# Low parts, half-length convolution filters and per-token roots in a split-float32 hybrid layer

## The chip, the cores and the metric

The kernel runs on one core of a Trainium2 chip. The metric is device time in microseconds (us) of one execution. TensorE (PE in the profile) multiplies matrices into PSUM, which has eight banks of 128 x 512 float32 here. VectorE (DVE), ScalarE (ACT) and GpSimd (POOL) work element by element. SyncE (SP) issues most DMAs; GpSimd issues those that add while they copy. Each engine takes its instructions strictly in the order in which they were written.

## The reference

One layer over x, 1024 tokens x 1024 channels, all float32:

```python
u = x @ w_in + b_in                      # q k v z_att glu_a glu_b z_conv g_att g_conv
att = stick_breaking_attention(q, k, v)  # 8 heads of 64, strictly causal
att_branch = (att * silu(z_att)) @ w_att_proj
c = causal_depthwise_conv(glu_a * sigmoid(glu_b), conv_w) + conv_b   # 31 taps, 512 channels
c = silu(layer_norm(c, conv_ln_g, conv_ln_b))
conv_branch = (c * silu(z_conv)) @ w_conv_proj + b_conv_proj
y = (sigmoid(g_att) * att_branch + sigmoid(g_conv) * conv_branch) @ w_out
return layer_norm(2 ** 0.25 * x + y, ln_g, ln_b)
```

`att_branch`, `conv_branch` and both gates have 1024 channels, everything else in the branches has 512.

## The kernel before

Channels lie on partitions and tokens along the free axis (tiles of 128 x 1024, "blk"; half tiles of 128 x 512, "hf"). A float32 product is made of three faster ones: each operand is split into a rounded high part (`wh`, `xh`) and the rest, the low part (`wl`, `xl`), and `mm3` (lines 190 to 193) issues high x high, high x low, low x high for each 128-channel slice. A weight piece is 128 x 512; `feed` keeps at most `N_SPL` = 5 split pieces at once, so a piece can be split at most four pieces before its use. ScalarE makes `wh` (line 216). The low part is made in one of three ways: VectorE or GpSimd subtracts, or ScalarE writes minus `wh` (line 222) and GpSimd issues a DMA that adds the weight from memory (line 223).

The order of work: the values of the attention (pieces 0 to 7), then attention units on TensorE with the input projection's remaining pieces (8 to 53, "dense work") laid between them, then `p12` pieces (36 to 39, 42, 43 and 54 to 67). The two gates and z_conv, 20 column blocks of w_in, go in ten pairs; each pair is a seven-product scheme. Two products use plain weights (`p12`), the other five (`P5 P6 P7 P4 P3`, pieces 68 to 117, results in `sps`) use sums and differences that `make_s` forms on VectorE: S1, then S2 from S1, then S4 from S2, all in the same half tile `s`, and S3; A22 is plain. `split_operand` (line 899 issues the DMA) splits them; `DMA_LOW` names those whose low part is made by the adding DMA. Each of `pair_out`'s sums is a VectorE addition that reads PSUM and frees a bank. Then follow the attention's projection (pieces 118 to 125, operands `ach`, `acl`), the convolution's (126 to 133, operands `cch`, `ccl`) and the output projection.

In the dense work VectorE also does the depthwise convolution: `conv_block` has one 128 x 1024 instruction per tap (line 387, 31 for each of four channel blocks). When all blocks are done `conv_norm` sums over channels on TensorE (lines 601, 602, `mps` and `vps`, each source split into two parts first), and takes the reciprocal root of the variance as 128 x 1024, the same on every partition. `ev_qk` evacuates q and k of a head in two halves of 64 partitions each.

What sets the order is a planner: `Timeline` holds a price per engine and instruction; `tl.run` writes each instruction of VectorE, ScalarE and GpSimd into its queue when the planner's clock says that the engine is free, by rank (convolution taps have rank 9, last). The order is fixed when the program is built; on the chip only semaphores act.

Of the kernel before, what the change touches and what calls it, by code (L numbers as in the profile page):

```python
# [9 lines left out]
F32 = mybir.dt.float32  # L10
# [4 lines left out]
P = 128  # L15
# [3 lines left out]
H = 8  # L19
# [22 lines left out]
DMA_LOW = ("A22", "S3", "S4")  # L42

A_LOW, C_LOW, O_LOW = "V", "G", "V"

# [10 lines left out]
GUARD = 150  # L56

# [100 lines left out]
def layer_kernel(ctx: ExitStack, tc, xT, x, wv, wd, wa, wc, wo, vec, bv, lng, lnb, cst, out):  # L158
# [30 lines left out]

    def mm3(ps, wh, wl, mh, ml, first, last):  # L190
# [7 lines left out]
    epsc = const.tile([P, 1], F32, name="epsc")  # L198
    ones = const.tile([P, P], F32, name="ones")
# [86 lines left out]
    def run_dense():  # L286
        for n_item, (first_piece, npc, mov, evac, may, nhf) in enumerate(items):
            dstat["item"] = n_item
            nk = 4 * npc
            if mov is None:  # L290
# [4 lines left out]
                for k in range(nk):  # L295
                    if k % 4 == 0:
                        while live["ps"] >= 8:
                            tl.skip()
                        ps = bank("dps")
                    pi = first_piece + k // 4  # L300
                    need(pi)
                    wh, wl = parts[pi]
                    kk = slice((k % 4) * P, (k % 4 + 1) * P)
                    mm3(ps, wh[:, kk], wl[:, kk], xh[k][:, 0:HALF], xl[k][:, 0:HALF], k % 4 == 0, k % 4 == 3)
                    tl.t += 3 * pe_ns(HALF)
                    if k % 4 == 3:
                        parts.pop(pi)
                        stat["free"] += 1
                        feed()
                        evac(ps, None if k == 3 else ps)  # L310
                    yield
            for half in range(2 if mov is not None else 0):
# [6 lines left out]
                for k in range(nk):  # L319
                    pi = first_piece + k // 4  # L320
                    need(pi)
                    wh, wl = parts[pi]
                    kk = slice((k % 4) * P, (k % 4 + 1) * P)
                    mh, ml = mov(k)
                    mm3(ps, wh[:, kk], wl[:, kk], mh[:, cols], ml[:, cols], k == 0, k == nk - 1)
                    tl.t += 3 * pe_ns(HALF)
                    if half == 1 and k % 4 == 3:
# [3 lines left out]
                    if k == nk - 1:  # L331
# [57 lines left out]
    def ev_qk(h):  # L389
        def f(half, cols, ps):  # L390
            if half == 0:
                qhh[h], qll[h], ks[h] = (blk(f"{n}{h}", F32R) for n in ("qhh", "qll", "ks"))
                qk_left[h] = [6, 2, 0.0]
            else:
                qk_left[h][1] = 2
            lo, up = slice(0, DH), slice(DH, P)
            a, b, c = qhh[h], qll[h], ks[h]
            left = qk_left[h]
            mine = [2]

            def fin(e):
                left[0] -= 1
                left[2] = max(left[2], e)
                if left[0] == 0:
                    qk_ready[h] = left[2]

            def read(e):
                mine[0] -= 1
                if mine[0] == 0:
                    drop("ps")  # L410

            def dup():
                fin((yield act(2, a[up, cols], f32(a[lo, cols]))))

            def q():
                e = yield act(0, a[lo, cols], ps[lo], AF.Identity, bias=vcol(h, lo))
                tl.spawn(dup(), e)
                e = yield vstt(0, b[lo, cols], ps[lo], vcol(h, lo), f32(a[lo, cols]), ALU.add, ALU.subtract)
                read(e)
                fin((yield act(2, b[up, cols], f32(b[lo, cols]))))  # L420

            def k():
                yield act(0, c[up, cols], ps[up], AF.Identity, bias=vcol(h, up))
# [933 lines left out]
```

## Time and profile before

| | |
|---|---|
| median of 3 runs | 794.17 us (790.4 to 795.58) |
| profiled execution | 791.7 us, span 789.8 us |
| PE busy | 749.3 us (95%) |
| DVE busy | 659.5 us (83%) |
| ACT busy | 398.4 us (50%) |
| POOL busy | 107.5 us (14%) |
| DMA moved | 109.55 MB |

A matmul's busy time contains its way through the array, so matmuls overlap and a busy share of 95% hides idle time; the spacing of their starts tells more. On DVE and ACT, too, an instruction's recorded time reaches into the next one's. The span has five stages: values (0 to 60 us), attention with dense work (60 to 340), the rest of the dense work (340 to 400), `p12` and the pairs (400 to 620, where the attention's projection begins near 601), the projections and the output (620 to the end).

### The profile page before, as it was taken

How to read it: one execution, taken by the hardware profiler on the slowest of the kernel's cores; microseconds unless marked ns; L12 is line 12 of the kernel's file. 1: busy time of each engine (PE TensorE's matmuls, PEld its weight loads, DVE VectorE, ACT ScalarE, POOL GpSimd, SP SyncE). 2: the span in 40 equal slices, each digit the busy share in tenths (PEclk: the TensorE clock that was granted, in tenths of full speed). 3: DMA queues.
4: the chain of work that ended last, by engine and by line, in shares of the span. 5: the costliest groups of instructions: out<-in, count | busy, mean ns of one | idle time of the engine just before them, and what ended most of it. 6: DMA issues, size and time to landing. Idle time of an engine off the chain costs nothing.

```text
span 789.8 us, 10242 instructions
## 1 busy us (share of the span) xinstructions
PE 749.3 (95%) x3606; PEld 624.0 (79%) x3606; DVE 659.5 (83%) x877; ACT 398.4 (50%) x747; POOL 107.5 (14%) x176
## 2 busy tenths in 40 slices
PE   9999999999999999999998989888977999999995
PEld 7887888888878888888876777667765888888885
DVE  7456989999999999979999998989899858920885
ACT  2159865975587898725525353346655334300100
POOL 3212001110110111011212111111110022100000
PEclk9999999999999999999999999999999999999998
DMA  7535125222432334396769767767667777140052
GB/s 245 159 67 117 33 40 107 54 55 54 109 78 50 85 79 114 70 298 186 199 148 247 187 170 175 201 179 193 158 155 258 263 245 260 68 173 0 1 187 80
DMA packets 49730, 109.55 MB, mean 139 GB/s; under 512 B 5520, under 2 KB 6416, under 8 KB 49680
## 3 DMA queue, kind: packets, MB, share of 16 engines
q1 hardware_dynamic: 36864, 85.77, 32.0%
q0 software_dynamic: 12672, 23.07, 18.1%
q8 instruction: 28, 0.46, 0.2%
q14 instruction: 22, 0.18, 0.1%
q10 hardware_dynamic: 144, 0.07, 0.0%
HBM read 84.24 MB, written 19.40 MB: 131 GB/s over the span
## 4 chain that ended last, share of the span: by engine, by line
PE 62%; issue 13%; DVE 13%; DMA 5%; ACT 4%; POOL 2%; SPq 0%; POOLq 0%; DVEq 0%; ACTq 0%
PE dps L192 10%; PE dps L191 10%; PE dps L193 10%; PE vps L1116 6%; PE yps L192 4%; PE yps L193 4%; PE yps L191 4%; DVE cacc L387 4%; PE pvps L754 4%; PE tps L731 3%; DMA wl<-s 3%; PE sps L193 2%; PE sps L191 2%; PE sps L192 2%; DVE f L713 2%
## 5 line engine op out<-in xcount | busy, mean ns | idle before, releaser
L193 PE MATMUL dps<-xh,wl 128*128 128x512 f32 x400 | 156.9, 392 | 5.0 <-DMA wl<-wd 5.0
L191 PE MATMUL dps<-xh,wh 128*128 128x512 f32 x400 | 157.8, 395 | 0.0
L192 PE MATMUL dps<-xl,wh 128*128 128x512 f32 x400 | 156.6, 392 | 0.0
L387 DVE SCALAR_TENSOR_TENSOR cacc<-cin,vecs,cacc 128x1023 f32<-128x1023 f32 (+24 forms) x120 | 148.1, 1270 | 0.7
L223 POOL DMA_DIRECT2D wl<-wd x58 | 50.4, 869 | 318.4 <-ACT wl L222 254.1
L193 PEld LDWEIGHTS dps<-xh,wl 128*128 128x128 f32 x400 | 75.4, 189 | 22.1 <-DMA wl<-wd 5.9
L713 DVE TENSOR_TENSOR_SCAN f<-f,eyez 128x896 f32<-128x896 f32 (+3 forms) x64 | 84.5, 1344 | 3.4 <-ACT f L381 3.4
L192 PEld LDWEIGHTS dps<-xl,wh 128*128 128x128 f32 x400 | 75.6, 189 | 14.0
L191 PEld LDWEIGHTS dps<-xh,wh 128*128 128x128 f32 x400 | 75.5, 189 | 13.8
L216 ACT ACTIVATE wh<-wr 128x512 fp32r<-128x512 f32 x84 | 53.2, 633 | 63.4 <-DMA wr<-wv 25.1
L192 PE MATMUL yps<-wol,mh 128*128 128x512 f32 (+1 forms) x136 | 51.2, 377 | 0.0
L193 PE MATMUL yps<-woh,ml 128*128 128x512 f32 (+1 forms) x136 | 51.2, 376 | 0.0
L191 PE MATMUL yps<-woh,mh 128*128 128x512 f32 (+1 forms) x136 | 51.2, 376 | 0.0
L381 ACT ACTIVATE wth<-tps 128x384 fp32r<-128x384 f32 (+1 forms) x80 | 41.4, 563 | 17.1 <-PE tps L731 15.6
L384 DVE TENSOR_TENSOR wtl<-tps,wth 128x384 fp32r<-128x384 f32 (+1 forms) x80 | 47.1, 627 | 2.9 <-ACT wth L381 2.5
L381 ACT ACTIVATE f<-zps 128x384 f32<-128x384 f32 (+2 forms) x96 | 45.0, 515 | 4.9 <-PE zps L699 4.4
L384 DVE TENSOR_TENSOR b<-b,f 128x895 f32<-128x895 f32 (+3 forms) x64 | 46.7, 747 | 0.3
L387 DVE SCALAR_TENSOR_TENSOR xrow<-xrow,yps 128x512 f32<-128x512 f32 (+1 forms) x17 | 10.7, 655 | 43.0 <-PE yps L193 42.7
L381 ACT ACTIVATE b<-zps 128x383 f32<-128x383 f32 (+2 forms) x96 | 46.0, 529 | 0.3
L220 POOL TENSOR_TENSOR wl<-wr,wh 128x512 fp32r<-128x512 f32 x18 | 25.8, 1434 | 106.0 <-ACT wh L216 101.1
L754 PE MATMUL pvps<-wth,v 128*128 128x256 f32 (+1 forms) x160 | 40.0, 279 | 0.0
L754 PE MATMUL pvps<-wtl,v 128*128 128x256 f32 (+1 forms) x160 | 39.8, 286 | 0.2 <-DVE wtl L384 0.2
(173 smaller groups left out, 1658.3 us busy)
## 6 DMA issues: line engine op xcount, KB each, us to landing
wl<-wd POOLq DMA_DIRECT2D x68, 256.0 KB, 4.8
wr<-wd SPq DMA_DIRECT2D x60, 256.0 KB, 3.1
rc<-wd SPq DMA_DIRECT2D x20, 512.0 KB, 7.2
c<-c SPq DMA_DIRECT2D x30, 256.0 KB, 2.8
ga<-c SPq DMA_DIRECT2D x8, 512.0 KB, 5.5
wor<-wo SPq DMA_DIRECT2D x16, 256.0 KB, 4.5
gc<-c SPq DMA_DIRECT2D x8, 512.0 KB, 5.6
xrow<-x SPq DMA_DIRECT2D x8, 512.0 KB, 6.5
```

The lines of the kernel that those rows point to most:

```text
L191: nc.tensor.matmul(ps, wh, mh, start=first, stop=False)
L192: nc.tensor.matmul(ps, wh, ml, start=False, stop=False)
L193: nc.tensor.matmul(ps, wl, mh, start=False, stop=last)
L216: yield "A", 1, HALF, lambda: nc.scalar.activation(wh, r, AF.Copy)
L220: e = yield "G", 0, HALF, lambda: nc.gpsimd.tensor_tensor(wl, r, f32(wh), op=ALU.subtract)
L223: e = yield "G", 0, 0, lambda: nc.gpsimd.dma_start(wl, src, accum_op=ALU.add), {"extra": 430}
L381: return "A", u, n, (lambda: nc.scalar.activation(out, in_, func, **kw)), (BIAS if "bias" in kw else {})
L384: return "V", u, n, lambda: nc.vector.tensor_tensor(out, a, b, op=op)
L387: return "V", u, n, (lambda: nc.vector.scalar_tensor_tensor(out, a, s, b, op0, op1)), (PTR if ptr else {})
L713: yield ("V", 2, n, lambda: nc.vector.tensor_tensor_scan(f[:, 0:n][:, ::-1], f[:, 0:n][:, ::-1], eyez[:, S - n:S][:, ::-1], 0.0, op0=ALU.mult,
L754: nc.tensor.matmul(u.ps[:, 0:n], st, wt[:, jj * 256:jj * 256 + n], start=(i == m and jj == 0 and wt is wh), stop=(i == 0 and jj == 1 and w ...
L1116: nc.tensor.matmul(vps[tb], a[k][:, tt], b, start=k == 0 and j == 0, stop=k == NK - 1 and j == 2)
```

## The change

Eight edits are made together. `DMA_LOW` becomes empty and VectorE makes the low parts of all pair operands; the same holds for the last 14 plain pieces before the pairs (54 to 67, `N_TURN`). `mm_piece` takes the place of `mm3` in the projections: per piece first the eight products with `wh`, then the four with `wl`. `ev_qk` makes one high and one low part for q and k together on 128 partitions, then four copies of 64 partitions. The convolution runs on even and odd tokens: three half-length filters (even tokens with 16 even taps, odd tokens with 15 odd taps, their sum with the 16 sums of neighbouring taps, which are made once in `hs_`), from which the two output halves are combined; `cin` and `cacc` hold the even tokens in the first half. The norm's channel sums use unsplit float32 matmuls; the variance is summed per token (8 matmuls of one column), the root is taken on 128 x 8, and 8 diagonal tiles and two matmuls spread it over the partitions again (`rps`). `LAG` shifts these sums by 8 us on the planner's clock. Two GLU items move ahead of `p12` item 2, and the last two pairs are interleaved.

```diff
-DMA_LOW = ("A22", "S3", "S4")
+DMA_LOW = ()
+N_TURN, T_LOW = 14, "V"
+LAG = 8000
...
+    def mm_piece(ps, wh, wl, movs, first, last):
+        ks = [slice(k * P, (k + 1) * P) for k in range(4)]
+        for kk, (mh, ml) in zip(ks, movs):
+            nc.tensor.matmul(ps, wh[:, kk], mh, start=first and kk is ks[0], stop=False)
+            nc.tensor.matmul(ps, wh[:, kk], ml, start=False, stop=False)
+            tl.t += 2 * pe_ns(HALF)
+            yield
+        for kk, (mh, ml) in zip(ks, movs):
+            nc.tensor.matmul(ps, wl[:, kk], mh, start=False, stop=last and kk is ks[3])
...
         j = i - (len(pieces) - 2 * NK)
+        if 0 < items[n_pairs[0]][0] - len(pair_order) - i <= N_TURN:
+            return T_LOW
...
-            def q():
-                e = yield act(0, a[lo, cols], ps[lo], AF.Identity, bias=vcol(h, lo))
-                tl.spawn(dup(), e)
-                e = yield vstt(0, b[lo, cols], ps[lo], vcol(h, lo), f32(a[lo, cols]), ALU.add, ALU.subtract)
...
-            def k():
-                yield act(0, c[up, cols], ps[up], AF.Identity, bias=vcol(h, up))
-                e = yield vstt(0, c[lo, cols], ps[up], vcol(h, up), f32(c[up, cols]), ALU.add, ALU.subtract)
...
+            def g():
+                yield act(0, a[:, cols], ps, AF.Identity, bias=vcol(h))
+                yield vstt(0, b[:, cols], ps, vcol(h), f32(a[:, cols]), ALU.add, ALU.subtract)
+                drop("ps")
+                yield [act(2, c[up, cols], f32(a[up, cols])), act(2, c[lo, cols], f32(b[up, cols]))]
+                e = yield [act(2, a[up, cols], f32(a[lo, cols])), act(2, b[up, cols], f32(b[lo, cols]))]
...
-        yield "V", 9, S, lambda: nc.vector.tensor_scalar(a, c, w(0), vcol(CONVB + i), op0=ALU.mult,
-                                                         op1=ALU.add), {"per": 0.521}
-        for sh in range(1, TAPS):
-            yield vstt(9, a[:, sh:], c[:, :S - sh], w(sh), a[:, sh:], ALU.mult, ALU.add, S - sh, ptr=False)
...
+        def run(x, taps, y, prep=None):
+            if prep is not None:
+                yield prep
+            for m, h in enumerate(taps):
+                if m == 0:
+                    yield "V", 9, HALF, lambda: nc.vector.tensor_scalar(y, x, h, None, op0=ALU.mult), {"per": 0.521}
+                else:
+                    yield vstt(9, y[:, m:], x[:, :HALF - m], h, y[:, m:], ALU.mult, ALU.add, HALF - m, ptr=False)
...
+        def last():
+            yield vtt(9, b[:, ev], b[:, ev], a[:, ev], ALU.subtract)
+            yield vtt(9, a[:, 1:HALF], a[:, 1:HALF], a[:, HALF:S - 1], ALU.add, HALF)
+            yield vtt(9, a[:, od], b[:, ev], a[:, od], ALU.subtract)
+            yield "V", 9, S, lambda: nc.vector.tensor_scalar(a, a, vcol(CONVB + i), None, op0=ALU.add), {"per": 0.521}
...
+        tl.spawn(run(c[:, ev], [w(2 * m) for m in range(n)], a[:, ev]), tl.now)
+        tl.spawn(run(c[:, od], [w(2 * m + 1) for m in range(n - 1)], a[:, od]), tl.now)
+        tl.spawn(run(b[:, od], [hsum[:, m:m + 1] for m in range(n)], b[:, ev],
+                     vtt(9, b[:, od], c[:, ev], c[:, od], ALU.add)), tl.now)
...
-                nc.tensor.matmul(ps, ones_r, h[:, c], start=True, stop=False)
-                nc.tensor.matmul(ps, ones_r, l[:, c], start=False, stop=True)
+                nc.tensor.matmul(ps, ones, src[:, c], start=True, stop=True)
...
+                nc.tensor.matmul(ps[:, b:b + 1], q[:, b * P:(b + 1) * P], ones[:, 0:1], start=b == 0, stop=b == NT - 1)
...
-        yield "V", 1, S, lambda: nc.vector.reciprocal(r, sd), {"per": 6.2}
+        yield "V", 1, NT, lambda: nc.vector.reciprocal(r, sd), {"per": 6.2}
...
+        yield [("V", 1, P, (lambda b=b: nc.vector.tensor_scalar(dg[:, b * P:(b + 1) * P], ident, r[:, b:b + 1], None,
+                                                               op0=ALU.mult)), {"per": 0.521}) for b in range(NT)]
+        yield lambda: got.extend(total(dg, "rps"))
...
-    pair_order = [(q, n) for n in range(len(pairs)) for q in ("P5", "P6", "P7", "P4", "P3")]
+    n2 = len(pairs) - 2
+    pair_order = [(q, n) for n in range(n2) for q in ("P5", "P6", "P7", "P4", "P3")] + \
+        [(q, n) for qs in (("P5", "P6"), ("P7", "P4", "P3")) for n in (n2, n2 + 1) for q in qs]
...
-    p12_item(2)
-    att_done = lambda: flags["att"]
-    glu_item(2, lambda: heads_z_done(H - 1))
+    att_done = lambda: flags["att"]
+    z_done = lambda: heads_z_done(H - 1)
+    glu_item(2, z_done)
+    glu_item(3, z_done)
+    p12_item(2)
     zatt_item(3)
-    glu_item(3, att_done)
...
+        taps = vecs[:, w0:w0 + TAPS][:, ::-1]
+        nc.vector.tensor_tensor(hsum[:, 0:TAPS // 2], taps[:, 0:TAPS - 1:2], taps[:, 1:TAPS:2], op=ALU.add)
+        nc.vector.tensor_copy(hsum[:, TAPS // 2:], taps[:, TAPS - 1:TAPS])
```

How instructions move is shown at three places. First TensorE at piece 72, the first `P3` (operand S4; `xh`, `xl` are the split input). Before:

```order
L191 MATMUL sps_4630<-xh4_289,wh72_4529 128x512
L192 MATMUL sps_4630<-xl4_290,wh72_4529 128x512
L193 MATMUL sps_4630<-xh4_289,wl72_4530 128x512
L191 MATMUL sps_4630<-xh5_319,wh72_4529 128x512
L192 MATMUL sps_4630<-xl5_320,wh72_4529 128x512
L193 MATMUL sps_4630<-xh5_319,wl72_4530 128x512
```

and now:

```order
L199 MATMUL sps_4709<-xl6_363,wh72_4609 128x512
L198 MATMUL sps_4709<-xh7_392,wh72_4609 128x512
L199 MATMUL sps_4709<-xl7_393,wh72_4609 128x512
L203 MATMUL sps_4709<-xh4_290,wl72_4610 128x512
L203 MATMUL sps_4709<-xh5_320,wl72_4610 128x512
L203 MATMUL sps_4709<-xh6_362,wl72_4610 128x512
```

`wl72` was read by the third matmul of the piece and is read by the ninth now.

Second, GpSimd's queue at the turn from the dense work to the pairs. Before, it issues an adding DMA for each plain piece and for three of five pair operands:

```order
L223 DMA wl65_4352<-wd 128x512
L223 DMA wl66_4377<-wd 128x512
L223 DMA wl67_4404<-wd 128x512
L899 DMA wl70_4478<-rc25_3726 128x512
L899 DMA wl71_4503<-wd 128x512
L899 DMA wl72_4530<-s0_3729 128x512
L899 DMA wl75_4603<-rc27_4014 128x512
```

and now:

```order
L242 DMA wl51_3991<-wd 128x512
L242 DMA wl52_4017<-wd 128x512
L242 DMA wl53_4087<-wd 128x512
L239 TENSOR_TENSOR wl126_6071<-wr126_6006,wh126_6070 128x512
L239 TENSOR_TENSOR wl127_6124<-wr127_6075,wh127_6123 128x512
L239 TENSOR_TENSOR wl128_6169<-wr128_6096,wh128_6168 128x512
```

From piece 54 to piece 125 GpSimd has no low part to make; its queue has 121 rows where it had 165.

Third, VectorE at the first pair (`s0` holds S1, S2, S4 in turn; `rc24`, `rc25` are the pair's raw weights; `cacc`, `cs` are convolution sums). Before:

```order
L384 TENSOR_TENSOR wl69_4454<-s0_3729,wh69_4453 128x512
L387 SCALAR_TENSOR_TENSOR cacc3_4219<-cin3_4129,vecs_75,cacc3_4219 128x1014
L384 TENSOR_TENSOR c11_8_4486<-dps_4457,p1_8_4461 128x512
L384 TENSOR_TENSOR s0_3729<-rc24_3725,s0_3729 128x512
L387 SCALAR_TENSOR_TENSOR cacc2_3930<-cin2_3857,vecs_75,cacc2_3930 128x1004
```

and now:

```order
L396 TENSOR_TENSOR wl69_4535<-s0_3770,wh69_4534 128x512
L399 SCALAR_TENSOR_TENSOR cs3_4410<-cs3_4410,hs__77 128x508
L396 TENSOR_TENSOR s0_3770<-rc24_3766,s0_3770 128x512
L396 TENSOR_TENSOR c11_8_4566<-dps_4537,p1_8_4540 128x512
L396 TENSOR_TENSOR wl70_4560<-rc25_3767,wh70_4559 128x512
L399 SCALAR_TENSOR_TENSOR cacc3_4409<-cin3_4068,vecs_75,cacc3_4409 128x506
L399 SCALAR_TENSOR_TENSOR c11_8_4566<-c11_8_4566,vecs_75,zg200_4573 128x512
L399 SCALAR_TENSOR_TENSOR cacc3_4409<-cin3_4068,vecs_75,cacc3_4409 128x506
L396 TENSOR_TENSOR wl71_4583<-rc25_3767,wh71_4582 128x512
```

The low parts 70, 71 (and 72) are new in the queue; the taps are half as long, and the convolution's block 3, the only one still open, stands at about the sixth tap of each filter, where before blocks 2 and 3 stood at taps 20 and 10 of 30.

## Rows read from the trace of the kernel before

**Rows 1.** Busy time by window: step, then PE, PEld, DVE, ACT, POOL busy (instructions), granted clock, DMA share, GB/s.

```profile
60.00:340.00 280.00, 277.27 (x1551) 239.96 (x1550) 266.58 (x332) 215.93 (x451) 34.07 (x100) 1.00 0.35 78
340.00:400.00 60.00, 60.00 (x267) 49.67 (x266) 52.33 (x59) 25.49 (x40) 10.41 (x12) 1.00 0.80 224
400.00:620.00 220.00, 192.35 (x809) 152.26 (x808) 198.07 (x245) 105.99 (x170) 33.08 (x38) 0.98 0.72 194
620.00:780.00 160.00, 160.00 (x726) 133.26 (x725) 101.74 (x176) 31.22 (x55) 12.36 (x8) 1.00 0.39 137
440.00:520.00 80.00, 72.17 (x309) 56.86 (x308) 69.76 (x90) 31.34 (x55) 13.00 (x15) 1.00 0.70 181
```

**Rows 2.** Waits of TensorE: who waited for what, us in total, times, the longest.

```profile
PE sps L193 <- DMA wl<-s: 12.3, 8, 4.6
PE dps L193 <- DMA wl<-wd: 5.0, 2, 3.9
PE dps L192 <- DVE acl L384: 4.2, 3, 2.6
PE mps L602 <- DVE lnsl L384: 3.0, 1, 3.0
PE sps L193 <- DMA wl<-wd: 2.5, 3, 1.9
...
PE vps L602 <- DVE lnvl L384: 0.5, 1, 0.5
```

**Rows 3.** TensorE's instructions in order of time, 508 to 512 us: start, duration, line, output and inputs, [idle before].

```profile
508.97 0.39 PE L191 MATMUL sps<-tbh,wh 128*128 128x512 f32 x1
509.20 0.39 PE L192 MATMUL sps<-tbl,wh 128*128 128x512 f32 x1
511.48 0.50 PE L193 MATMUL sps<-tbh,wl 128*128 128x512 f32 x1 [1.89 <-DMA wl<-wd]
```

**Rows 4.** Windows (columns as in rows 1) around the two longest of these waits.

```profile
416.00:423.00 7.00, 5.66 (x18) 4.49 (x19) 7.00 (x7) 4.66 (x9) 2.00 (x3) 0.76 0.96 237
580.00:587.00 7.00, 4.89 (x15) 3.95 (x16) 5.30 (x8) 2.40 (x3) 0.00 (x0) 0.76 0.97 248
```

**Rows 5.** All engines in order of time: one S4 from its making to its use.

```profile
574.33 0.69 DVE L384 TENSOR_TENSOR s<-rc,s 128x512 f32<-128x512 f32 x1
...
575.13 0.63 ACT L381 ACTIVATE wh<-s 128x512 fp32r<-128x512 f32 x1 [1.35 <-DVE s L384]
...
576.19 0.62 ACT L381 ACTIVATE wl<-s 128x512 fp32r<-128x512 f32 x1
...
577.53 0.90 POOL L899 DMA_DIRECT2D wl<-s  x1
...
582.11 0.80 PE L193 MATMUL sps<-xh,wl 128*128 128x512 f32 x1 [4.61 <-DMA wl<-s]
```

**Rows 6.** VectorE in order of time; a row with x4 joins four instructions, and the next row's start gives the spacing.

```profile
397.89 0.75 DVE L387 SCALAR_TENSOR_TENSOR cin<-dps,vecs,sg 128x512 f32<-128x512 f32 x1
398.55 4.80 DVE L387 SCALAR_TENSOR_TENSOR cacc<-cin,vecs,cacc 128x997 f32<-128x997 f32 x4
403.26 0.76 DVE L387 SCALAR_TENSOR_TENSOR cin<-dps,vecs,sg 128x512 f32<-128x512 f32 x1
...
408.62 0.69 DVE L384 TENSOR_TENSOR c<-dps,p 128x512 f32<-128x512 f32 x1
409.22 0.82 DVE L575 TENSOR_SCALAR cacc<-cin,vecs 128x1024 f32<-128x1024 f32 x1
409.94 4.85 DVE L387 SCALAR_TENSOR_TENSOR cacc<-cin,vecs,cacc 128x1014 f32<-128x1014 f32 x4
```

**Rows 7.** Groups by line and shape: name, count, busy us, mean ns of one, idle before.

```profile
L387 DVE SCALAR_TENSOR_TENSOR ks<-dps,vecs,ks 64x512 fp32r<-64x512 f32 x16 | 12.1, 755 | 0.5
L387 DVE SCALAR_TENSOR_TENSOR qll<-dps,vecs,qhh 64x512 fp32r<-64x512 f32 x16 | 11.9, 742 | 7.8 <-ACT ks L381 7.6
L381 ACT ACTIVATE qll<-qll 64x512 fp32r<-64x512 f32 x16 | 10.1, 629 | 2.2 <-DVE qll L387 1.9
L384 DVE TENSOR_TENSOR wl<-s,wh 128x512 fp32r<-128x512 f32 x20 | 13.8, 689 | 0.0
L1107 DVE CAST xh<-xr 128x512 fp32r<-128x512 f32 x14 | 7.6, 546 | 3.1 <-DMA xr<-xT 3.1
L384 DVE TENSOR_TENSOR vraw<-vps,bvt 128x512 f32<-128x512 f32 x8 | 5.5, 691 | 13.4 <-PE vps L1116 13.4
L1108 DVE TENSOR_TENSOR xl<-xr,xh 128x512 fp32r<-128x512 f32 x14 | 12.6, 902 | 0.5
```

**Rows 8.** The same view: the norm's instructions that go.

```profile
L626 DVE RECIPROCAL lnr<-lnsd 128x1024 f32<-128x1024 f32 x1 | 6.5, 6547 | 0.0
L384 DVE TENSOR_TENSOR lnsl<-lnsum,lnsh 128x1024 fp32r<-128x1024 f32 x1 | 1.2, 1218 | 0.0
L387 DVE SCALAR_TENSOR_TENSOR lnsd<-vps,epsc,lnsd 128x512 f32<-128x512 f32 x2 | 1.4, 747 | 0.0
L601 PE MATMUL mps<-lnsh,ones_r 128*128 128x512 f32 x2 | 0.8, 392 | 0.0
```

**Rows 9.** TensorE at the start, in order of time: seven unsplit float32 matmuls of 128 columns, two records each.

```profile
1.06 3.35 PE L1092 MATMUL vps<-ones 128*128 128x128 f32 x14 [1.06 <-DVE ones L200]
4.34 1.11 PE L1116 MATMUL vps<-wh,xh 128*128 128x512 f32 x2
```

More of the change, by code (lines that the diff above doesn't have):

```diff
@@ L288, in run_dense @@
             dstat["item"] = n_item
-            nk = 4 * npc
             if mov is None:
@@ L294, in run_dense @@
                 dstat["in"] = True
[L295 to L300, printed above, removed]
-                    need(pi)
[L302 to L310, printed above, removed]
+                for j in range(npc):
+                    while live["ps"] >= 8:
+                        tl.skip()
+                    ps = bank("dps")
+                    pi = first_piece + j
+                    need(pi)
+                    movs = [(xh[k][:, 0:HALF], xl[k][:, 0:HALF]) for k in range(4 * j, 4 * j + 4)]
+                    yield from mm_piece(ps, *parts.pop(pi), movs, True, True)
+                    stat["free"] += 1
+                    feed()
+                    evac(ps, None if j == 0 else ps)
                     yield
@@ L318, in run_dense @@
                 dstat["in"] = True
-                for k in range(nk):
-                    pi = first_piece + k // 4
+                for j in range(npc):
+                    pi = first_piece + j
                     need(pi)
[L322 to L327, printed above, removed]
+                    movs = [[m[:, cols] for m in mov(k)] for k in range(4 * j, 4 * j + 4)]
+                    yield from mm_piece(ps, *parts[pi], movs, j == 0, j == npc - 1)
+                    if half == 1:
                         parts.pop(pi)
@@ L629, in conv_norm, with variances @@
-        drop("ps", 2)
-        yield "V", 1, S, lambda: nc.vector.tensor_scalar(sd, sd, -0.5, 1.5, op0=ALU.mult, op1=ALU.add), {"per": 0.521}
-        yield vtt(1, r, r, sd, ALU.mult, S)
-        left = [NC]
+        def variances():
+            ps = bank("vps")
+            for b in range(NT):
+                nc.tensor.matmul(ps[:, b:b + 1], q[:, b * P:(b + 1) * P], ones[:, 0:1], start=b == 0, stop=b == NT - 1)
+                tl.t += 4 * 109
+            return ps
+        got.clear()
+        yield tl.now + LAG
@@ new lines, in conv_norm @@
+        yield lambda: got.append(variances())
+        vps = got[0]
+        lt = blk("lnt")
+        sd, r, t2 = (lt[:, k * NT:(k + 1) * NT] for k in range(3))
+        yield "A", 0, NT, lambda: nc.scalar.activation(sd, vps[:, 0:NT], AF.Sqrt, bias=epsc[:, 0:1]), {"extra": 1300}
+        yield "V", 1, NT, lambda: nc.vector.reciprocal(r, sd), {"per": 6.2}
+        yield vtt(1, t2, r, r, ALU.mult, NT)
+        yield vstt(1, t2, vps[:, 0:NT], epsc[:, 0:1], t2, ALU.add, ALU.mult, NT)
+        drop("ps")
@@ L1002, in run_pairs @@
             need(pi)
-            wh, wl = parts.pop(pi)
-            for k in range(NH):
-                kk = slice(k * P, (k + 1) * P)
-                while name in ("P4", "P5", "P6", "P7") and (k not in t12 or k not in t34):
-                    tl.skip()
-                mh, ml = mov[name](k)
-                mm3(ps, wh[:, kk], wl[:, kk], mh, ml, k == 0, k == NH - 1)
-                tl.t += 3 * pe_ns(HALF)
-                if k == NH - 1:
-                    stat["free"] += 1
-                    feed()
-                    pp[n][name] = (ps, tl.t + 165)
-                    if n == len(pairs) - 1 and name in att_at:
-                        for p in att_at[name]:
-                            tl.spawn(split_att(p), tl.t)
-                yield
+            while name in ("P4", "P5", "P6", "P7") and (len(t12) < NH or len(t34) < NH):
+                tl.skip()
+            yield from mm_piece(ps, *parts.pop(pi), [mov[name](k) for k in range(NH)], True, True)
+            stat["free"] += 1
+            feed()
+            pp[n][name] = (ps, tl.t + 165)
+            if n == len(pairs) - 1 and name in att_at:
+                for p in att_at[name]:
+                    tl.spawn(split_att(p), tl.t)
+            yield
         flags["pairs"] = True
```

112 lines of the change are left out of this document (53 added, 59 removed).

## The prediction

> **What bounds the kernel now.** I read the windows by stage first [rows 1]. From 340 to 400 us TensorE runs 267 matmuls in 60 us, one per 0.225 us, without a break; the last stage runs as densely. That spacing is the floor of one 128x512 product, so a piece of twelve takes 2.70 us. From 400 to 620 us there are only 809 matmuls in 220 us: 809 x 0.225 = 182, so 38 us are lost there, in the pairs and the pieces before them. TensorE is the engine that sets the end and these 38 us are nearly all that this change can win.
>
> The waits of TensorE say where they go [rows 2]. Waits for a low part made by the adding DMA come to 12.3 + 5.0 + 2.5 = 19.8 us; for the attention's low part `acl` 4.2; for the norm's split sums 3.0 + 0.5. The instructions in order of time show the form of such a stop [rows 3]: high x high and low x high of one slice run, then the third matmul stands for 1.89 us. Two of the stops are followed by a stretch at the lower granted clock: windows of 7 us around them have a mean of 0.76 [rows 4], which is 7 x 0.24 = 1.7 us lost in each, 3.4 in all, at 1.2 instead of 2.4 GHz. Named so far: 19.8 + 4.2 + 3.5 + 3.4 = 30.9 us. The other 7 us lie in gaps too short to be told apart.
>
> One S4 shows why the DMA is late [rows 5]: made on VectorE at 574.33, high part at 575.13, ScalarE's copy at 576.19, issued by GpSimd at 577.53, used at 582.11. From the high part's start to the use are 7 us, of which 4.6 are TensorE's wait.
>
> VectorE is the next bound. It is busy for 266.6 of 280 us in the attention and for 198 of 220 in the pairs [rows 1]. What it can take is read from spacings, not durations [rows 6]: four taps of about 995 elements start within 4.71 us, 1.18 each, a 128x512 two-operand sum takes 0.60, one with a pointer scalar 0.66 (397.89 to 398.55), a one-operand pass of 1024 elements 0.72.
>
> **Part by part.** *Low parts.* The 30 pair operands and 14 plain pieces lose ScalarE's second copy, GpSimd's issue and the DMA, and get one VectorE subtraction each: 44 x 0.60 = 26.4 us on VectorE. In the chain above the low part would stand 0.6 us behind the high part, near 576.4, before TensorE comes at 577.3. TensorE also asks for it only at the ninth product of a piece, 6 x 0.225 = 1.4 us later than now. So the 19.8 us of DMA waits go, and with them the stops that brought the low clock, 3.4 us. What is late next is VectorE itself, below.
>
> *Convolution.* Before, a block takes 0.72 + 30 x 1.18 = 36.1 us. Now 44 taps of some 504 elements. No row has such a tap; above it is bounded by 0.76, the whole duration of the 64-row form of q and k [rows 7], below by 0.59, half of a long tap [rows 6]. The nearest row is the 128x512 form with a pointer, 0.66; eight elements fewer make 0.65. That gives 28.6, three first taps at some 0.45 (the 128x512 cast lasts 0.55 [rows 7]), four sums of 0.60 and one pass of 0.72: 33.1 us. Four blocks save 12 us of VectorE; by the ends of the tap's price they cost 7 more or save 23. Writing `cin` and reading `cacc` at a step of two elements I cost at nothing; at worst the 16 instructions double, 10 us.
>
> The Trainium skill, VectorE: DVE Perf Modes, "The DRAIN you can't avoid", says that the next operation does not start until the pipe has emptied, which would charge each instruction its whole duration; it adds that an operation that is not held starts earlier. By the whole durations a short tap would cost 0.74 and a block 38 of today's 39, so that the convolution would save 4 us in all, not 12. The trace speaks for the exception: four taps of 1.27 us start within 4.71 us.
>
> *q and k.* Per half, two VectorE instructions of 64 rows (0.74 and 0.76 [rows 7]) become one of 128 rows, 0.66: 16 x 0.84 = 13 us less on VectorE in the attention. ScalarE gets one copy of 0.63 more per half, 10 us on top of 215.9 in 280 us [rows 1]; units of a head wait for these copies. I charge 1 us, between 0 (ScalarE is 77% busy) and 5 (half of the copies seen).
>
> *The norm.* VectorE loses the reciprocal of 1024 columns, 6.5, two splits of 1.2, two instructions of 0.7 and three more full passes, about 13 us [rows 8]; it gets eight diagonal tiles of some 0.25, a few single columns and half passes, about 3. TensorE pays: `mps` and `rps` are four unsplit products of 512 columns. The only such rows are seven of 128 columns at the start, 3.35/7 = 0.48 each [rows 9]; 512 columns lie between one split product, 0.225, and four times that, 1.9. I take four passes, 0.9 each: 3.6 us, and 1.6 for the eight one-column products (0.2 each, between 0.12, half a record of these rows, and 0.48). The eight split products that go were 1.8. Net +3.4 us, with ends of 0 and +10. The waits for split sums, 3.5 us, go, since the sums are taken 8 us later by the planner's clock and need no split.
>
> *Order.* The eight short instructions that sum neighbouring taps stand before the evacuation of the values, where VectorE waits 13.4 us for TensorE [rows 7]: nothing. The attention's operands are split after `P6` of the last pair; three pieces followed it before, six follow now that the last two pairs are interleaved. `acl` comes 8 us earlier and its 4.2 us wait goes. GLU items come earlier, so the convolution ends sooner: at the first pair one block is open where there were two.
>
> *VectorE's pace.* Between the low parts of pieces 68 and 99 its queue now holds 146 instructions: 105 of 0.60, 34 short taps of 0.65, two of 0.66, four full sums of 1.13 and one pass, 91.7 us. TensorE needs 31 x 2.70 + 1.8 = 85.5 in the same stretch. VectorE falls 6 us behind, and with five slots its lead is at most four pieces, 10.8 us; after piece 99 it has less than TensorE (74 instructions, 42 us for 18 pieces of 48.6). The stall is therefore 0 if VectorE enters with its full lead and never waits; if it waits as often as it does now from 440 to 520 us (10.2 of 80 us idle [rows 1]) it is 6 + 12 - 10.8 = 7. I take 7, the upper one, as a queue that mixes six chains in a fixed order seldom keeps its lead.
>
> **Sum.** Waits on DMA -19.8, clock -3.4, norm's waits -3.5, `acl` -4.2, 2 of the 7 short gaps: -32.9. Norm's products +3.4, VectorE's pace +7, q and k +1: +11.4. Together -21.5 against the profiled execution's 791.7 us: 770.2. The median of the runs shown, 794.17, is 2.5 above that execution, so I forecast **773 us** on the scale of the median.
>
> **The rivals.** *VectorE never holds TensorE*: the pace term falls away and the short gaps go too, 773 - 7 - 5 = 761. For it: 42 us for 48.6 after piece 99, and the convolution's earlier end. Chance 0.15.
>
> *VectorE takes the place of the DMA.* Low parts, evacuations and sums for two pairs stand in one queue at over 95% load. If its idle share of now stays and the lead is small when the pairs begin, the stall is 18 us; two low-clock stretches come back with it: 773 - 7 + 18 + 3.4 = 787, and 792 with 5 us more lost in the attention by late copies. For it: the present 90% [rows 1]; against it: the sum of VectorE's work is some 10 us less than now. TensorE would wait for VectorE low parts and sums. Charging whole durations in the same stretch (146 x 0.085 = 12 us more) leads to the same time. Chance 0.22.
>
> The rule of the Trainium skill named above (VectorE: DVE Perf Modes, "The DRAIN you can't avoid") would bring that about by itself; by the spacings shown it has 0.03 of that chance.
>
> *Slower, by the price of a tap.* If a short tap costs 0.84 instead of 0.65 (the 128x512 subtraction of the first stage lasts 0.90 where others last 0.69 [rows 7], so such a form exists), 176 taps cost 33 us more on an engine that is busy 95% in the attention. Nothing there hides it: the taps stand ahead of evacuations in a fixed queue. 773 + 33 - 4 of lead = 802; it decides from about 0.80 per tap on. Chance 0.07.
>
> *The change does not do what it says*: excluded for the DMA, whose rows are gone from GpSimd's queue; that the low parts were never the cause, so that TensorE stops for the same S4 by another path (its making at 574.33 is itself late), would leave 794: 0.02.
>
> **Numbers.** The forecast, 764 to 781, has 0.54; 0.15 + 0.22 + 0.07 + 0.02 are as above. About 1% (786 and 802) is what a measurement of this kernel can tell from no change. Faster: 0.54 + 0.15 + half of the second rival = 0.80; within 1%: the other half, 0.02 and a little of the slow case, 0.14; slower 0.06. The range leaves out the lower third of the best case, 0.05, and what lies above 790, some 0.15: 760 to 790.
>
> **What would show it.** Right: no wait of TensorE on a DMA for `wl` from 400 us on, over 920 matmuls in that stage's 220 us, clock 1.00 there; short taps spaced 0.65; VectorE at 90% or more between the first pair and the norm's mean, with TensorE's longest waits there on VectorE. Wrong: taps at 0.75 or more; unsplit products of over 1.2 us; a wait of TensorE on `mps`, `vps` or `rps` sources; waits in the attention on ScalarE's copies of q and k.

## The result and the profile after

The changed kernel takes **765.91 us** (median; 764.16 to 767.2), the kernel before 793.57 beside it: a ratio of 0.965 with an interval of 0.961 to 0.969, 27.7 us. The forecast was 773 with a range of 760 to 790. The profiled execution took 767.04 us, span 765.0, against 791.7 and 789.8.

The windows by stage of the changed kernel (columns as in [rows 1]), with two short ones at the end:

```profile
60.00:340.00 280.00, 277.09 (x1542) 238.16 (x1541) 264.22 (x369) 220.75 (x462) 33.08 (x98) 1.00 0.34 73
340.00:400.00 60.00, 60.00 (x267) 49.67 (x266) 55.15 (x82) 24.18 (x35) 6.04 (x7) 1.00 0.65 195
400.00:620.00 220.00, 216.10 (x942) 175.77 (x941) 209.27 (x339) 93.86 (x149) 4.04 (x3) 0.99 0.53 178
440.00:520.00 80.00, 80.00 (x349) 65.00 (x348) 79.89 (x129) 28.71 (x47) 0.00 (x0) 1.00 0.47 155
...
517.00:524.00 7.00, 5.63 (x24) 4.04 (x23) 7.00 (x12) 3.37 (x5) 0.00 (x0) 1.00 0.16 59
584.00:591.00 7.00, 6.33 (x21) 5.03 (x22) 7.00 (x12) 1.27 (x2) 0.00 (x0) 0.76 0.79 271
```

From 400 to 620 us TensorE now runs 942 matmuls where [rows 1] has 809; the attention (1542 after 1551) gained nothing. VectorE is busy for 79.89 of 80 us from 440 to 520, after 69.76. GpSimd's 33.08 us of that stage have become 4.04.

TensorE's waits, the same view as [rows 2]:

```profile
PE dps L199 <- DVE acl L396: 2.5, 3, 1.0
...
PE sps L203 <- DVE wl L396: 1.3, 1, 1.3
```

No wait on a DMA is left in the pairs, and none on the norm's sums; one on a low part that VectorE makes, and part of the wait on `acl`.

The instructions in order of time show what remains (start, duration, engine, line, output and inputs, [idle before]). First VectorE's low part and TensorE's use of it, for piece 68 and for piece 99; between them the two unsplit products of the norm's mean (two records each); last the attention's operand:

```profile
430.64 0.68 DVE L396 TENSOR_TENSOR wl<-s,wh 128x512 fp32r<-128x512 f32 x1
...
435.52 0.84 PE L203 MATMUL sps<-tah,wl 128*128 128x512 f32 x3
...
502.67 1.90 PE L617 MATMUL mps<-lnsum,ones 128*128 128x512 f32 x4
504.00 0.79 PE L198 MATMUL sps<-tah,wh 128*128 128x512 f32 x1
504.63 0.39 PE L199 MATMUL sps<-tal,wh 128*128 128x512 f32 x1
...
522.77 0.68 DVE L396 TENSOR_TENSOR wl<-s,wh 128x512 fp32r<-128x512 f32 x1
...
523.50 1.19 PE L203 MATMUL sps<-tah,wl 128*128 128x512 f32 x4 [1.28 <-DVE wl L396]
...
580.93 0.68 DVE L396 TENSOR_TENSOR acl<-attb,ach 128x512 fp32r<-128x512 f32 x1
581.53 0.74 DVE L399 SCALAR_TENSOR_TENSOR c<-c,vecs,zg 128x512 f32<-128x512 f32 x1
582.20 0.68 DVE L396 TENSOR_TENSOR acl<-attb,ach 128x512 fp32r<-128x512 f32 x1
582.80 1.22 DVE L396 TENSOR_TENSOR cacc<-cacc,lng 128x1024 f32<-128x1024 f32 x1
583.93 0.68 DVE L396 TENSOR_TENSOR acl<-attb,ach 128x512 fp32r<-128x512 f32 x1
...
584.67 0.50 PE L199 MATMUL dps<-acl,wh 128*128 128x512 f32 x1 [1.00 <-DVE acl L396]
```

Piece 68 is ready at 431.32, 4.2 us before its use; piece 99 at 523.45, and TensorE has stood 1.28 us for it. So VectorE's lead is used up inside the pairs. The last three of eight `acl` stand in VectorE's queue between a sum's gate (`zg`) and the norm's last steps (`lng`).

The taps, VectorE in order of time and the groups (line, shape, count, busy us, mean ns):

```profile
408.26 0.73 DVE L399 SCALAR_TENSOR_TENSOR cs<-cs,hs__77 128x500 f32<-128x500 f32 x1
408.91 1.38 DVE L399 SCALAR_TENSOR_TENSOR cacc<-cin,vecs,cacc 128x498 f32<-128x498 f32 x2
410.21 0.68 DVE L237 TENSOR_TENSOR wl<-wr,wh 128x512 fp32r<-128x512 f32 x1
```

```profile
L399 DVE SCALAR_TENSOR_TENSOR cacc<-cin,vecs,cacc 128x504 f32<-128x504 f32 x8 | 5.7, 735 | 0.0
L399 DVE SCALAR_TENSOR_TENSOR cin<-dps,vecs,sg 128x512 f32<-128x512 f32 x8 | 5.9, 740 | 0.3 <-PE dps L203 0.3
```

Three taps start within 1.95 us, 0.65 each.

The convolution's last low parts (line, tile, count, shortest, median and longest ns, first and last start):

```profile
L396 DVE TENSOR_TENSOR ccl<-zs,cch x8: 678/680/1192, 600.6 to 612.5; 128x512 fp32r<-128x512 f32 x8
```

TensorE's first use of them starts at 625.9, so the convolution ends with 25 us to spare for the first.

### The profile page after: what moved, and what is told of

The parts are those of the page before. It is cut to its first block, busy times and chain, and to the rows that moved or that the text cites. A ratio compares the mean times of both kernels' runs of the same rounds, so it can differ in the third digit from the quotient of the medians.

```text
span 765.0 us, 10211 instructions
## 1 busy us (share of the span) xinstructions
PE 748.2 (98%) x3622; PEld 625.4 (82%) x3622; DVE 651.3 (85%) x1006; ACT 379.7 (50%) x716; POOL 69.5 (9%) x132
## 4 chain that ended last, share of the span: by engine, by line
PE 58%; DVE 25%; ACT 9%; issue 6%; DMA 2%; SPq 0%; DVEq 0%; ACTq 0%
PE dps L203 11%; PE dps L198 11%; PE dps L199 11%; PE vps L1145 6%; DVE cacc L399 4%; PE yps L209 4%; PE yps L210 4%; PE yps L211 4%; PE pvps L790 3%; PE tps L767 3%; DVE cs L399 2%; DVE wl L396 2%; DVE c L396 2%; DVE cacc L396 2%; DVE u L396 2%
## 5 line engine op out<-in xcount | busy, mean ns | idle before, releaser
L203 PE MATMUL dps<-xh,wl 128*128 128x512 f32 x400 | 109.0, 391 | 0.0
L399 DVE SCALAR_TENSOR_TENSOR cacc<-cin,vecs,cacc 128x511 f32<-128x511 f32 (+14 forms) x116 | 82.4, 735 | 0.1
L242 POOL DMA_DIRECT2D wl<-wd x44 | 38.2, 868 | 271.7 <-ACT wl L241 240.8
L399 DVE SCALAR_TENSOR_TENSOR cs<-cs,hs__77 128x511 f32<-128x511 f32 (+14 forms) x60 | 44.1, 735 | 0.1
```

Of the source, the lines that this page charges most:

```text
L203: nc.tensor.matmul(ps, wl[:, kk], mh, start=False, stop=last and kk is ks[3])
L399: return "V", u, n, (lambda: nc.vector.scalar_tensor_tensor(out, a, s, b, op0, op1)), (PTR if ptr else {})
```

## The experiments

The theory after the result: the adding DMA was what TensorE waited for, and the change gains by taking it away; the other edits are worth what room they make on VectorE. The rivals: the route alone is the gain and the rest is idle time of an engine with time to spare; or the new order of products and pieces is the gain. Each experiment is the changed kernel with one part put back or altered, if nothing else is said; "above" is the distance of its median from 765.91. Beside the runs without the shift, with the old order of pairs, with the old order of products ahead of the pairs, and of the full form again, the kernel before took 795.0, 1.4 more than beside the changed kernel; by the ratios the distance of the first two is smaller by about as much, and the gain of the last two larger. The earlier GLU items were put back in no run.

**The adding DMA back for three pair operands and for the last 14 plain pieces.**

```diff
-DMA_LOW = ()
+DMA_LOW = ("A22", "S3", "S4")
-N_TURN, T_LOW = 14, "V"
+N_TURN, T_LOW = 0, "V"
```

> The changed kernel with the adding DMA back for A22, S3 and S4 of each pair and for the last 14 plain pieces; all else as changed. If the DMA route was what TensorE waited for, its waits on the DMA come back, less the 1.4 us per stop that the new order inside a piece hides: 8 to 20 us slower than the changed kernel, 774 to 786 us, with waits of TensorE on DMA wl of 6 to 15 us and the lower clock in at least one stretch. If instead the new order inside a piece or the earlier convolution made the gain, 766 to 769 us and DMA waits under 2 us.

Measured: 785.27 us, ratio 0.989 (0.985 to 0.992), 19.4 us above the changed kernel. Its waits, and the windows of the longest of them:

```profile
PE sps L203 <- DMA wl<-wd: 6.8, 2, 4.2
PE dps L203 <- DMA wl<-wd: 3.2, 4, 2.0
PE yps L209 <- DVE tc L399: 2.8, 3, 1.0
```

```profile
541.00:548.00 7.00, 2.80 (x10) 1.98 (x9) 7.00 (x11) 4.86 (x7) 1.52 (x2) 0.74 1.00 249
548.00:555.00 7.00, 7.00 (x26) 5.62 (x25) 7.00 (x12) 3.58 (x6) 1.06 (x2) 0.78 0.65 167
```

The waits on the DMA are back, and a clock below 1.00 after the longest. They are 10.0 us where [rows 2] has 19.8, though: `wl` is used later now (by the ninth product of a piece, not the third), and VectorE has more room; which of the two hides the rest was not tried apart. These waits are about half of the loss. Another 2.8 us stand in the output (`yps`). The windows of 7 us from 403 to 704 us fall short of a clock of 1.00 by 10.3 us in sum, where the changed kernel loses 1.7 (an estimate: 7 us times what is missing to 1.00 in each). Less the 3.8 us of waits on `wl` and `acl` that only the changed kernel has, that makes 17.6 of the 17.9 us between the two profiled spans. Of the parts put back one at a time the route costs most.

**The route alone**: the kernel before, with VectorE low parts and nothing else of the change.

```diff
-DMA_LOW = ("A22", "S3", "S4")
+DMA_LOW = ()
+N_TURN, T_LOW = 14, "V"
```

> The kernel before with one edit: all pair operands' low parts and those of the last 14 plain pieces by VectorE. If the route alone matters and VectorE has room even with the old convolution, q/k and norm, 770 to 776 us, TensorE's waits on low parts under 4 us in all. If the room has to be made first (VectorE gets 26 us of work with nothing taken away), VectorE holds TensorE in the pairs: 780 to 792 us, with waits of TensorE on wl made by VectorE of 5 us or more and low parts ready less than 1 us ahead.

Measured: 799.39 us, ratio 1.008 (1.005 to 1.010), 5.6 us slower than before and slower than either expectation.

```profile
PE dps L193 <- ACT cch L385: 19.2, 1, 19.2
PE mps L605 <- ACT lnsh L385: 8.7, 1, 8.7
```

```profile
500.00:620.00 120.00, 107.38 (x449) 86.95 (x448) 116.30 (x156) 47.59 (x75) 1.86 (x1) 0.93 0.47 165
```

The waits on the DMA are gone, and those on VectorE's `wl`, of which I had expected 5 us or more, are 1.9. But VectorE is full to the end of the stage. The planner puts taps last, so the convolution pays: the norm's sum and then `cch`, the operand of the convolution's projection, come late. The first rival falls: the route without the room is worth nothing.

**The old convolution**: full-length taps, tokens in their natural order.

```diff
-        tl.spawn(run(c[:, ev], [w(2 * m) for m in range(n)], a[:, ev]), tl.now)
...
+        for sh in range(1, TAPS):
+            yield vstt(9, a[:, sh:], c[:, :S - sh], w(sh), a[:, sh:], ALU.mult, ALU.add, S - sh, ptr=False)
```

> The changed kernel with the convolution before: 31 taps of full length, tokens in their natural order, one block at a time. VectorE gets back 3 us per block, 12 in all, about 6 of them after 380 us where it is busy without a break. If the shrinking lead is the right picture (8 us at piece 57, 2.9 at piece 90), 6 us more leave TensorE waiting some 3 us: 767 to 772 us. If VectorE has room to spare, 766 us as now; if a short tap is not cheaper than half a long one and the edit bought nothing, VectorE's busy time does not rise.

Measured: 778.75 us, ratio 0.981 (0.978 to 0.985), 12.8 us above, more than expected.

```profile
PE dps L198 <- ACT cch L393: 13.9, 1, 13.9
PE dps L199 <- DVE ccl L396: 1.2, 1, 1.2
```

VectorE's busy time is 667.6 us after 651.3, and the pairs stay dense. The loss stands in one place, at the convolution's projection, as in the kernel with the route alone:

```profile
L396 DVE TENSOR_TENSOR ccl<-cacc,cch x8: 680/682/684, 633.6 to 640.3; 128x512 fp32r<-128x512 f32 x8
```

The low parts come 33 us later than in the changed kernel, which had 25 to spare. That is twice the 16 us of added work, and the norm's first sum comes 52 us later (550.0 after 498.3). The planner gives taps only what other work leaves, and a block is one chain of taps here instead of three; which of the two counts was not tried.

**The old norm**: split sums, the root on 1024 columns, no shift.

```diff
-                nc.tensor.matmul(ps, ones, src[:, c], start=True, stop=True)
+                nc.tensor.matmul(ps, ones_r, h[:, c], start=True, stop=False)
+                nc.tensor.matmul(ps, ones_r, l[:, c], start=False, stop=True)
...
-        yield tl.now + LAG
-        yield "V", 1, NT, lambda: nc.vector.reciprocal(r, sd), {"per": 6.2}
+        yield "V", 1, S, lambda: nc.vector.reciprocal(r, sd), {"per": 6.2}
```

> The changed kernel with the old norm: split sources, reciprocal of 1024 columns, no shift of the sums. VectorE gets 10 us more, TensorE 3.4 less, and the chain is without its three shifts of 8 us. If VectorE's room is what counts, the lead of 15 us at the convolution's projection swallows most of it, and TensorE waits for the split sums again: 766 to 772 us, with 3 to 8 us of waits on mps and vps sources. If the chain's length counts, it is as fast or faster, 761 to 766 us.

Measured: 779.18 us, ratio 0.983 (0.978 to 0.988), 13.3 us above: more than either expectation.

```profile
PE mps L623 <- ACT lnsh L393: 4.9, 1, 4.9
PE sps L198 <- ACT wh L393: 4.6, 2, 3.5
PE sps L203 <- DVE wl L396: 3.2, 2, 2.7
PE mps L624 <- DVE lnsl L396: 2.2, 1, 2.2
```

Of these waits half is the sums' own, half is late operands of the pairs. Which part of the edit keeps the first half away, the next run says.

**The new norm without the shift.**

```diff
-LAG = 8000
+LAG = 0
```

> The changed kernel without the 8 us by which the norm's sums are put later on the planner's clock; its arithmetic stays new. If the 13 us that the old norm cost came from the missing shift (its products waited 4.9 and 2.2 us): waits on lnsum of 3 to 6 us, 769 to 774. If they came from VectorE's 13 us of more work: 764 to 767, wait on lnsum at most 2.

Measured: 772.88 us, ratio 0.972 (0.971 to 0.974), 7.0 us above.

```profile
PE mps L617 <- DVE lnsum L396: 7.2, 1, 7.2
```

```profile
502.00:509.00 7.00, 5.98 (x12) 3.45 (x13) 6.72 (x11) 1.17 (x2) 0.00 (x0) 0.56 0.18 68
```

As I read it, the planner believes the sum done some 7 us before VectorE has it, and writes the products where TensorE must stand. So about half of the old norm's 13 us is the missing shift; the rest goes with the old arithmetic and shows as the late `wh` and `wl` above, which this run does not have. Which of its instructions counts was not tried.

**The old evacuation of q and k**, two halves of 64 partitions.

```diff
-                yield act(0, a[:, cols], ps, AF.Identity, bias=vcol(h))
-                yield vstt(0, b[:, cols], ps, vcol(h), f32(a[:, cols]), ALU.add, ALU.subtract)
+                e = yield vstt(0, b[lo, cols], ps[lo], vcol(h, lo), f32(a[lo, cols]), ALU.add, ALU.subtract)
...
+                e = yield vstt(0, c[lo, cols], ps[up], vcol(h, up), f32(c[up, cols]), ALU.add, ALU.subtract)
```

> The changed kernel with q and k evacuated as before, in halves of 64 partitions. VectorE gets 13 us more in the attention and ScalarE 10 us less. If VectorE's room is what counts and the convolution gives way, the last low part of the convolution comes 13 us later against a lead of 15: 766 to 771 us. If ScalarE's copies cost something in the attention, it is faster there by 1 to 3 us: 763 to 766 us.

Measured: 767.47 us, ratio 0.967 (0.964 to 0.970), 1.6 us above, within the scatter. VectorE's busy time is 665.1 us, 14 more, and still nothing is lost:

```profile
L396 DVE TENSOR_TENSOR ccl<-zs,cch x8: 673/682/1181, 616.2 to 628.7; 128x512 fp32r<-128x512 f32 x8
```

The work pushes taps back and the convolution ends 16 us later, inside the 25 us to spare. Room on VectorE in the attention is worth little by itself.

**Every pair low part written twice** (the second writing repeats the first; the planner is not told).

```diff
-            e = yield vtt(1, wl, src, f32(wh), ALU.subtract)
+            def low():
+                for _ in range(2 if True else 1):
+                    nc.vector.tensor_tensor(wl, src, f32(wh), op=ALU.subtract)
+            e = yield "V", 1, HALF, low
```

> The changed kernel with each low part of the 50 pair operands written twice by VectorE: 30 us more work on VectorE between the first pair and the attention's projection, the planner not told. In the changed kernel the convolution's last low part stands about 15 us before its projection asks for it. If VectorE's room is used up at that far end, as the run with long taps showed, 778 to 785 us, with one wait of TensorE of 10 to 18 us on cch or ccl, and little in the pairs. If the low parts' own lead in the pairs decides, the waits lie on wl there, 10 us or more.

Measured: 802.52 us, ratio 1.011 (1.007 to 1.014), 36.6 us above, for 50 x 0.60 = 30 us of work.

```profile
PE sps L203 <- DVE wl L943: 13.2, 10, 2.4
PE dps L199 <- DVE acl L396: 4.7, 2, 4.2
PE sps L198 <- ACT wh L393: 4.7, 5, 1.9
```

I had expected a wait on `cch` and less loss. The order was fixed with the taps ahead of the low parts, so the pairs stand instead. Extra work on VectorE in the pairs came out at the end somewhat worse than one for one.

**The last two pairs one after the other**, as before.

```diff
-    pair_order = [(q, n) for n in range(n2) for q in ("P5", "P6", "P7", "P4", "P3")] + \
-        [(q, n) for qs in (("P5", "P6"), ("P7", "P4", "P3")) for n in (n2, n2 + 1) for q in qs]
+    pair_order = [(q, n) for n in range(len(pairs)) for q in ("P5", "P6", "P7", "P4", "P3")]
```

> The changed kernel with the last two pairs one after the other again, as before. My prediction's step (the wait on acl is a matter of how many pieces follow P6): acl is waited for 5 to 9 us instead of 2.5, 768 to 773. Rival (acl is late because VectorE's queue is full at that point, whatever the order of pieces): wait 1 to 4, 764 to 767.

Measured: 772.41 us, ratio 0.972 (0.970 to 0.973), 6.5 us above.

```profile
PE dps L199 <- DVE acl L396: 5.2, 5, 1.6
```

```profile
577.00:584.00 7.00, 4.49 (x12) 2.62 (x11) 7.00 (x13) 6.42 (x11) 0.00 (x0) 0.77 0.82 296
584.00:591.00 7.00, 4.30 (x12) 2.56 (x12) 7.00 (x11) 1.37 (x3) 0.00 (x0) 0.74 0.69 236
591.00:598.00 7.00, 7.00 (x26) 5.58 (x25) 3.85 (x7) 2.42 (x4) 0.00 (x0) 0.76 0.96 363
```

The order of the last pairs does decide how long `acl` is waited for: its last part starts at 588.8 us here, at 583.9 in the changed kernel. There are 2.7 us more of waits, and three windows at a clock of about 0.75 where the changed kernel has one.

**The three products of a slice together again**, all else changed.

```diff
             nc.tensor.matmul(ps, wh[:, kk], ml, start=False, stop=False)
-            tl.t += 2 * pe_ns(HALF)
-            yield
-        for kk, (mh, ml) in zip(ks, movs):
             nc.tensor.matmul(ps, wl[:, kk], mh, start=False, stop=last and kk is ks[3])
-            tl.t += pe_ns(HALF)
-            if kk is ks[1]:
+            tl.t += 3 * pe_ns(HALF)
+            if kk is not ks[3]:
                 yield
```

> The changed kernel with the three products of each slice together again, so that wl is asked for by the third matmul and not the ninth. The shortest lead of a low part in the changed kernel is 2.9 us at the ninth matmul, so about 1.5 us at the third: if leads decide, 0 to 2 us slower, 766 to 768 us. If the order inside a piece is a main part of the gain, 771 us or more with waits on wl of 4 us or more.

Measured: 760.44 us, ratio 0.958 (0.955 to 0.961): faster than the changed kernel by 5.5. To find where, the old order was put into the projections alone (pieces 118 to 133), then into everything ahead of the pairs alone, and the full form was timed again:

```diff
+        if dstat["item"] >= n_pairs[0] :
...
```

> The changed kernel with the three products of each slice together in the two branch projections alone (pieces 118 to 133); every queue up to there is the same. If the mixed order was faster because the high-first order runs through the attention's operands in 1.8 instead of 2.7 us and meets acl too early, the waits on acl (2.5 us) and the lower clock behind them go: 761 to 764 us. If the gain came from the planner's other interleaving before the pairs' end, 765 to 767 us and the waits on acl stay.

```diff
+        if "pairs" not in dstat:
...
     def run_pairs():
-        dstat["in"] = True
+        dstat["in"] = dstat["pairs"] = True
```

> The products of a slice stand together only ahead of the pairs (attention, gates, q and k); in the pairs and behind them all high parts come first, as in the changed kernel. If the lead of the fully mixed order comes from how the planner weaves VectorE's work in before the pairs: 759 to 762, VectorE busy for about 57.8 of 60 us from 340 to 400 (55.2 in the changed kernel), no wait on acl. If it comes from the pairs themselves: 764 to 767 with the wait on acl of 2 to 3 us.

> The changed kernel with the three products of a slice together again, a second time, with more rounds. If its lead over the changed kernel is real: 758 to 762 us, a ratio to the kernel before of 0.955 to 0.961, no wait of TensorE on acl above 0.6 us. If the first measurement was luck: 764 to 767, as the changed kernel.

Measured: in the projections alone 765.3 (0.964; 0.961 to 0.967), nothing; ahead of the pairs alone 761.49 (0.958; 0.956 to 0.960); in all pieces again 759.8 (0.956; 0.955 to 0.957). The kernel with the old order ahead of the pairs alone: its windows by stage, one window at the waits on `acl`, these waits, and its instructions in order of time:

```profile
60.00:340.00 280.00, 278.20 (x1551) 240.19 (x1550) 265.31 (x372) 220.28 (x463) 33.27 (x98) 1.00 0.34 77
340.00:400.00 60.00, 60.00 (x267) 49.67 (x266) 57.94 (x86) 24.33 (x37) 6.05 (x7) 1.00 0.61 183
```

```profile
577.00:584.00 7.00, 5.47 (x22) 3.88 (x23) 7.00 (x11) 1.58 (x3) 0.00 (x0) 1.00 0.81 298
```

```profile
PE dps L208 <- DVE acl L405: 1.8, 3, 1.0
```

```profile
426.18 0.68 DVE L405 TENSOR_TENSOR wl<-s,wh 128x512 fp32r<-128x512 f32 x1
...
433.47 0.84 PE L212 MATMUL sps<-tah,wl 128*128 128x512 f32 x3
```

Two things differ ahead of the pairs. The attention runs 1551 matmuls again, 2 us gained. And VectorE works 57.94 of 60 us where it worked 55.15, so that it enters the pairs with a lead of 433.47 - 426.86 = 6.6 us, not 4.2. That is enough for the low parts: this kernel has no wait on one in the pairs. I had expected that the wait on `acl` would go as well; 1.8 us of it stay, but no window of the pairs or the projection behind them is below a clock of 1.00. The 2 us of the attention, 1.3 of `wl`, 0.7 of `acl` and 1.7 of the clock make 5.7 of the 6.5 us between the profiled spans. With the edit the pauses inside a piece at which the planner places other engines' work (`yield`) fall differently; TensorE runs as densely from 340 to 400 us with either order of products, so I take the pauses as the cause, though no run separates the two. The version with the products together in every piece beats both kernels. The last of the rivals is half true: the order of pieces is worth 5 to 6.5 us, while the new order of products, as it was built, costs 4 to 6.

## Why the prediction was right, and where not

**Right:** the time within its range, the bound (TensorE's 38 us lost from 400 to 620), the cause (the adding DMA) and the sign. By the forecast's own count, 918 products at 0.225 fill 206.6 of the 220 us now, and the norm's unsplit ones 5.4 (four of 0.87, and eight of one column from 533.4 to 535.3): 8 us are lost where 38 were.

**Term by term**, against the profiled executions:

| term | forecast | measured |
|---|---|---|
| waits on DMA | -19.8 | -19.8 |
| lower clock | -3.4 | -1.7: the window from 584 stays at 0.76 |
| norm's split sums | -3.5 | -3.5 |
| `acl` | -4.2 | -1.7: 2.5 us stay |
| short gaps | -2 of 7 | -4.5: of the 8 us, 2.5 + 1.3 + 1.7 are named here, 2.5 are short gaps |
| norm's products | +3.4 | +3.6 |
| VectorE's pace | +7 | +1.3 |
| q and k | +1 | +2: nine matmuls fewer in the 280 us of the attention |

The measured terms make -24.3 and the two profiled spans differ by 24.8; the forecast's net was -21.5. That the net is so near is in part luck: pace and short gaps came out 8.2 us better than forecast, the clock, `acl`, the norm's products and the attention 5.4 us worse. The other half of the distance between 773 and 765.9 is scatter: the profiled execution of before stood 2.5 us under its median, that of after 1.1 over its own.

**The term that failed is VectorE's pace.** Its work was sized well: 146 instructions in 91.7 us forecast, 92.1 measured between the ends of the two low parts (431.32 to 523.45). The step "if it waits as often as it does now, 10.2 of 80 us idle" was wrong: that idle time in [rows 1] was TensorE's stops handed on to VectorE, and it went with them. The full lead of 10.8 us was wrong too, the other way; it was 4.2. With both put right, from what was measured afterwards, the step reads 6 - 4.2 = 1.8, and the wait is 1.3. So "VectorE never holds TensorE" (761) was nearly true of the low parts in the pairs as measured, and fully so in the kernel with 6.6 us of lead; `acl` holds TensorE in both. "VectorE takes the place of the DMA" (787) names what was close by: the two runs with more work on VectorE, the route alone and the doubled low parts, gave 799 and 803.

**`acl`** was half right. It comes earlier, from 568.1 us on instead of 578.2 with the old order of pairs. That the whole wait goes was wrong: three of eight stand behind other work in VectorE's queue, which the step had not looked at.

**The attention's loss** was put down to ScalarE's copies of q and k in the forecast. Its nine matmuls are back (1551) with these copies in place and the old order of products ahead of the pairs; with the old evacuation of q and k instead, five are back (1547). So the copies cost about 1 us at most, and the new order of products, which the forecast charged with nothing here, goes with the whole loss.

**The shift** of the norm's sums was one clause in the forecast ("taken 8 us later by the planner's clock"); it is worth 5.6 to 7 us by itself. The clause was right, its weight unseen, since [rows 2] shows only the 3.5 us that the old order lost.

**A short tap** starts every 0.65 us at a duration of 0.735, as forecast; the strided `cin` takes 740 ns after 750 to 760 in [rows 6], so the step of two elements costs nothing there. The Trainium skill, VectorE: DVE Perf Modes, "The DRAIN you can't avoid", would have charged the whole duration; the trace shows starts inside it, as it allows for operations that are not held. **An unsplit product** of 512 columns takes (504.63 - 0.23 - 502.67) / 2 = 0.87 us, counted to one spacing before the product at 504.63; forecast 0.9.

**The parts do not add up.** Put back one at a time they cost 19.4, 12.8, 13.3, 1.6 and 6.5 us, 54 together for a gain of 28. The route shows it most plainly: taken out of the whole it costs 19.4 us, put into the kernel before by itself it loses 5.6. I read this as VectorE's room in the same 220 us, which the convolution and the norm free and the route uses; no run puts back two parts at once.

## What to carry to other kernels

When work moves from a late DMA to an engine, ask first whether that engine has room in that very stage; the move alone was slower here, with the room it was the largest gain. Do not carry idle shares over from a trace in which the engine waits for the one that you are about to free: take the length of its queue and the lead with which it enters. And where a planner fixes the order, look ahead of the stage as well: the run with 2.8 us more of VectorE's work done before the pairs gained 4 to 6 us, while the order of products in the two projections alone, at the point of the wait on `acl`, gave nothing.

## What was not expected of the hardware

How much clock a stop costs. One stop of 1.28 us on TensorE (523.50) leaves the windows from 517 and 524 at 1.00. Three stops on `acl` of 0.5 to 1.0 us, 2.5 us in all, leave the window from 584 at 0.76 in the changed kernel, that is, part of it at 1.2 instead of 2.4 GHz. Three such stops of 1.8 us in all, the last of 1.00 as well, leave 1.00 in the kernel with the old order of products ahead of the pairs; where the difference lies no run shows. A stop of 7.2 us leaves 0.56, and the four unsplit records of the mean, 1.90 us in the changed kernel, took 3.78 there:

```profile
503.02 3.78 PE L617 MATMUL mps<-lnsum,ones 128*128 128x512 f32 x4 [7.20 <-DVE lnsum L396]
```
